# Attention stage of a hybrid layer: two output products of a tile to steps 59 and 61, and its second square, root, norm and row transposes later

## The chip, the cores and the metric

The kernel is one program on one core of a Trainium2 chip. The metric is the device time of one execution in microseconds. It computes a whole transformer layer: modulation, retention, attention, output projection and feed-forward. The engines are TensorE (PE in the profile, its weight loads PEld), VectorE (DVE), ScalarE (ACT), GpSimd (POOL) and SyncE (SP), which issues the transfers.

## The reference

The layer has 2048 rows of width 1024, 256 context rows, 4 retention heads and 8 attention heads in 2 groups of 4 (each group has one key and value head). What matters here is the line that joins the two halves, and the normalised row that the feed-forward reads:

```python
ret = _ret_out(ret, rg, ret_gn_g)                       # retention, normalised and gated, 512 wide
att = _latent_attention(q, k, v, kc, vc)                # softmax(q k^T / 8) v over 2304 keys, 512 wide
x = x + g1 * (jnp.concatenate([ret, att], axis=-1) @ w_out)
h2 = _modulate(_rmsnorm(x, norm2_g), sh2, sc2)          # x * rsqrt(mean(x^2) + eps) * g * (1 + sc2) + sh2
x = x + g2 * _sqrelu_mlp(h2, w_ff1, w_ff2)
return _rmsnorm(x, final_norm_g)
```

## The kernel before

The rows are 16 tiles of 128, worked from t = 15 down to t = 0. The attention stage is one long list of **steps**. A planner, `on(k, phase, fn, ...)`, files each piece of work under a step and a phase; the stage then runs through the steps, in each through the phases `begin, scores, piece, maximum, early, exp, cast, low, chain, pe, values, late, dma`, and each piece adds its instructions to its engines' queues. So the table of steps is the order on every engine, and every engine works strictly in that order. Engines wait for each other by semaphores alone.

A head group of a tile has 18 steps, a tile 36. In every step attention does the following, for keys in blocks of 128 or 512:

- **scores** (L210, L211): two matmuls, 128x512, into one of two PSUM buffers `st`
- **piece** (L177 or two L181): one matmul of the next group's plain scores into one of two buffers `mp`, whose row maximum VectorE takes one step later (L190)
- **exp** (L216): ScalarE, one step later, `st` to `p`; every second step **cast** (L220) makes the fp16 part `phi`
- **low** (L227 on GpSimd, whole, or L229 on VectorE, two halves): the rest `plo`
- **values** (L242 to L245): every second step, 16 small matmuls of `phi` and `plo` with the values into `o`; at a group's end ScalarE takes `o` to `so` (L249, L250) and GpSimd makes `ma` (L262, L263).

Around this stand the other jobs of a tile, each with steps of its own. Let k = 40 + 36 n for the n-th tile; "step 59" of a tile means k + 59. So step 59 of one tile is step 23 of the next.

- `retention`: score (bank 0) at 2 (38 of the tile before), heads at 6 to 9 (42 to 45), copy `oo` at 46, statistics at 48 and 49, a root on GpSimd (cv_gn, mr, cy_gn, mr), four norms on ScalarE (L1696) at 52 and 54, the gate (L1700); the decays oqf and oqb (L1652, GpSimd) at 68 and 69, and a weighing okw (L1628).
- `output_tile`: transposes of the retention half `oo` at 24 and of the attention half `ma` at 28 (L1816), each split into fp16 parts (`rh`, `rl`, `ah`, `al`); then 16 products (L1834 to L1836, three matmuls each), 8 for each half of the 1024 columns, at the steps of the table `PLACES`, accumulated in PSUM bank 0; per half an `add` to the row `xr` (L1841, VectorE) and a `square` with a row sum (L1848, ScalarE); then the row goes out (`store_x`), a `root` of the sums (a VectorE add L1855, then two small GpSimd operations cv_f and cy_f, which a list called `chain` hands out one after each of three phases), a `norm` of the row in place (L1861, GpSimd), eight transposes in two lots (L1866), `modulate` (L1871, VectorE), `shift_` (L1876, GpSimd) and two stores of the new row `h2`.
- `parts` and `turn` of attention: the row maxima of the next group go through three small GpSimd operations (mt, L198 to L200) at 50 and 68 into four VectorE transposes (L204) at 52 and 70.
- `h_pair`: from the eighth tile on, rows of finished tiles are read back and combined: GpSimd sums (L1933) and fp16 splits (ScalarE L72, GpSimd L73), more of them in every second tile, where a pair begins.

The last tile (t = 0) has a table of its own, `LAST`.

Of the kernel before, what the change touches and what calls it, by code (L numbers as in the profile page):

```python
# [56 lines left out]
def layer_kernel(ctx: ExitStack, tc: tile.TileContext, a: dict, out: bass.AP):  # L57
# [84 lines left out]
    early = kp.tile([P, NK * (VW + 1)], F32, name="early", tag="wv")  # L142
# [127 lines left out]
    with ExitStack() as st, tc.manual_schedule():  # L270
# [952 lines left out]
        for n, (col, s) in enumerate(((C_RK, 5), (C_AKV, 6), (C_AQ, 12), (C_RQ, 16), (C_RV, 18), (C_RG, 26))):  # L1223
            w = weights[0, col]
            for j in range(w.n):
                at = s + (j if col != C_RV else j > 0)
# [35 lines left out]
        at = [16, 17, 18, 19, 20, 20, 21, 21, 24, 25, 39, 40, 41, 42, 44, 46, 49, 50, 52, 54, 56, 58, 60, 62]  # L1262
# [3 lines left out]
        at = [39, 40, 41] + list(range(43, 64, 2)) + list(range(66, 84))  # L1266
        for i in range(32):
            greatest_of(i, at.pop(0))
        at = list(range(7, 18)) + list(range(36, 42)) + [43, 46, 50, 54, 57] + list(range(66, 84))
# [265 lines left out]
    def on(k, phase, fn, *args):  # L1535
        events.setdefault((k, phase), []).append((fn, args))
# [262 lines left out]
        on(k + 3, "pe", spread)  # L1799
        on(k + 3, "late", scales)  # L1800

    PLACES = (28, 29, 30, 31, 32, 33, 34, 35, 46, 48, 49, 50, 52, 54, 55, 57)
    LAST = (23, 24, 25, 26, 30, 31, 32, 33, 25, 26, 27, 28, 34, 34, 35, 35)

    def output_tile(t, k, last):
# [78 lines left out]
            on(k + at[1], "cast", part, w, 0)  # L1884
            on(k + at[2], "low" if last and w == "a" else "early", part, w, 1)
        on(k + 26, "dma", fetch_x)
        places = LAST if last else PLACES
        for j, at in enumerate(places):
            on(k + at, "pe", product, j // 8, j % 8)
        for n in range(2):  # L1890
            at = k + places[8 * n + 7] + 1
            on(at, "early", add, n)
            on(at if last else at + 1, "cast", square, n)
        made = at
        on(made + 1, "dma", store_x)
        on(made if last else made + 2, "late", root)
        on(k + 68 if t == 1 else made + 2 if last else made + 4, "late", norm)
        if last:
            for f in (transpose_x, modulate, shift_, store_h):
                rest.extend([(f, 0), (f, 1)])  # L1900
# [1 line left out]
        if t == 1:  # L1902
# [3 lines left out]
                on(k + 82 + q, "late", shift_, q)  # L1906
                on(k + 83 + q, "dma", store_h, q)
            return made
        on(k + 68, "pe", transpose_x, 0)
        on(k + 70, "early", modulate, 0)  # L1910
        on(k + 72, "pe", transpose_x, 1)
        on(k + 73, "early", modulate, 1)
        for q in range(2):
            on(k + 74 + q, "late", shift_, q)
            on(k + 76 + q, "dma", store_h, q)
        return made


# [40 lines left out]
    for n, t in enumerate(range(NT - 1, -1, -1)):  # L1959
        made_at = output_tile(t, R0 + RF * n, n == NT - 1)  # L1960
# [449 lines left out]
    with tc.manual_schedule():  # L2410
# [8 lines left out]
        k = min(events)[0]  # L2419
# [69 lines left out]
```

## Time and profile before

| | |
|---|---|
| median of 3 runs | 2636.21 us (2634.91 to 2636.67) |
| profiled execution, first to last instruction | 2633.9 us (its time is given as this span alone) |
| granted TensorE clock, mean | 0.999 |
| busy: TensorE / VectorE / ScalarE / GpSimd | 98% / 78% / 57% / 67% |
| matmuls | 16617 |
| attention stage, first to last L210 | 598.0 to 1443.8 us |

The profile is of one execution. Busy times are sums over the span. A timeline row has a start in us from the span's start, a duration in us, engine, line, operation, output<-input, shapes and a count of merged instructions, and in brackets the idle time before it with what ended it. A matmul row of 512 columns shows 0.38 us, but the next one starts 0.216 us later, since matmuls overlap; so distances are read from start to start.

### The profile page before, as it was taken

To read this page: it belongs to the slowest core of one execution; us is meant where nothing else is said; L and a number is where in the kernel's file an instruction comes from. 1 tells how busy PE (TensorE), PEld (TensorE's weight loads), DVE (VectorE), ACT (ScalarE), POOL (GpSimd) and SP (SyncE) were. 2 spreads that over 40 slices of the span, in tenths; PEclk is the share of its full clock that TensorE was granted. 3 is DMA by queue.
4 is the path that set the end of the run, shared out by engine and by line. 5 is a ranking of instruction groups with operands and counts; after the bars stand their busy time and mean duration, and the time that the engine had idled before them with its cause. 6 is when DMAs were issued, how large, how long until landed. Compare 5 with 4: busy or idle time off the path is not lost.

```text
span 2633.9 us, 45447 instructions
## 1 busy us (share of the span) xinstructions
PE 2594.3 (98%) x16617; PEld 1450.6 (55%) x16617; DVE 2043.7 (78%) x3080; ACT 1509.5 (57%) x2562; POOL 1762.5 (67%) x1451
## 2 busy tenths in 40 slices
PE   8999999998999999999999999999999999999998
PEld 5875555546666666666666444444444444444443
DVE  5688898668888888888887697889886666656686
ACT  3865453427777787888788476656665322222243
POOL 3644566536676678798887695777662566666686
PEclk9999999999999999999999999999999999999999
DMA  7776999736122132333322855777784748475453
GB/s 232 274 255 214 312 328 340 257 106 220 49 71 59 57 112 74 101 85 115 99 83 75 293 159 163 233 224 232 223 293 139 281 170 300 163 284 185 151 190 114
DMA packets 332903, 481.84 MB, mean 183 GB/s; under 512 B 90228, under 2 KB 200068, under 8 KB 328200
## 3 DMA queue, kind: packets, MB, share of 16 engines
q1 hardware_dynamic: 332664, 478.94, 55.2%
q8 instruction: 130, 2.13, 0.3%
q14 instruction: 93, 0.76, 0.1%
q10 hardware_dynamic: 16, 0.01, 0.0%
HBM read 321.89 MB, written 156.38 MB: 182 GB/s over the span
## 4 chain that ended last, share of the span: by engine, by line
PE 84%; DVE 5%; ACT 4%; DMA 3%; POOL 2%; issue 2%; SPq 0%; DVEq 0%; POOLq 0%; ACTq 0%
PE pd L2302 7%; PE pd L2300 7%; PE pd L2301 7%; PE pu L2073 7%; PE pu L2075 7%; PE pu L2074 7%; PE pso L1193 4%; PE pso L1195 4%; PE pso L1194 4%; PE st L210 4%; PE o L245 4%; PE st L211 4%; PE mp L177 3%; PE o L243 2%; PE bank L1836 2%; PE bank L1834 2%
## 5 line engine op out<-in xcount | busy, mean ns | idle before, releaser
L190 DVE TENSOR_REDUCE nm<-mp 128x1 f32<-128x512 f32 x558 | 377.7, 685 | 89.2 <-PE mp L177 83.7
L216 ACT ACTIVATE p<-st 128x512 f32<-128x512 f32 x576 | 341.1, 599 | 154.4 <-PE st L211 150.5
L227 POOL TENSOR_TENSOR plo<-p,phi 128x1024 f16<-128x1024 f32 x160 | 347.0, 2174 | 86.2 <-ACT phi L220 86.1
L2073 PE MATMUL pu<-hf,w1f 128*128 128x512 f16 x896 | 339.6, 379 | 1.5 <-ACT w1f L2049 0.9
L2075 PE MATMUL pu<-hf,w1f 128*128 128x512 f16 x896 | 339.6, 379 | 0.4 <-DVE w1f L2055 0.4
L2300 PE MATMUL pd<-w,uf 128*128 128x512 f16 x896 | 339.6, 379 | 0.0
L2302 PE MATMUL pd<-w,uf 128*128 128x512 f16 x896 | 339.6, 379 | 0.0
L2301 PE MATMUL pd<-w,uf 128*128 128x512 f16 x896 | 339.6, 379 | 0.0
L2074 PE MATMUL pu<-hf,w1f 128*128 128x512 f16 x896 | 339.6, 379 | 0.0
L2320 POOL TENSOR_TENSOR y<-y,d 128x512 f32<-128x512 f32 x128 | 210.5, 1647 | 146.6 <-ACT uf L2289 95.5
L220 ACT ACTIVATE phi<-p 128x1024 f16<-128x1024 f32 x288 | 305.1, 1059 | 0.0
L229 DVE TENSOR_TENSOR plo<-p,phi 128x512 f16<-128x512 f32 x256 | 236.3, 924 | 21.2 <-ACT phi L220 8.7
L243 PE MATMUL o<-wv,plo 128*128 128x65 f16 x2304 | 230.0, 193 | 0.0
L245 PE MATMUL o<-wv,phi 128*128 128x129 f16 x2176 | 228.3, 220 | 0.0
L210 PE MATMUL st<-qr,ks 128*128 128x512 f16 x576 | 218.0, 379 | 8.7 <-ACT p L216 6.2
L243 PEld LDWEIGHTS <-plo 128*128 128x128 f16 x2304 | 205.1, 98 | 28.5 <-issue 0.6
L2312 DVE SCALAR_TENSOR_TENSOR y<-pd,scy,y 128x512 f32<-128x512 f32 x160 | 116.9, 747 | 131.8 <-PE pd L2302 130.4
L211 PE MATMUL st<-qr,ks 128*128 128x512 f16 x576 | 218.2, 379 | 0.1
L2085 DVE TENSOR_TENSOR r<-pu,r 128x512 f32<-128x512 f32 x224 | 150.0, 684 | 82.7 <-PE pu L2075 56.8
L1193 PE MATMUL pso<-wf,h_l 128*128 128x512 f16 (+1 forms) x576 | 208.1, 361 | 0.0
L1195 PE MATMUL pso<-wf,h_l 128*128 128x512 f16 (+1 forms) x576 | 208.1, 361 | 0.0
L1194 PE MATMUL pso<-wf,h_l 128*128 128x512 f16 (+1 forms) x576 | 208.1, 361 | 0.0
(394 smaller groups left out, 6118.0 us busy)
## 6 DMA issues: line engine op xcount, KB each, us to landing
wm<-in_w_ff SPq DMA_DIRECT2D x64, 512.0 KB, 6.4
u<-r SPq DMA_DIRECT2D x128, 256.0 KB, 4.3
ur<-u SPq DMA_DIRECT2D x128, 256.0 KB, 5.8
y<-x SPq DMA_DIRECT2D x64, 512.0 KB, 6.2
wf<-w2f SPq DMA_DIRECT2D x112, 256.0 KB, 2.8
w<-wf SPq DMA_DIRECT2D x28, 1024.0 KB, 9.8
w1r<-in_w_ff SPq DMA_DIRECT2D x48, 512.0 KB, 5.3
x<-y SPq DMA_DIRECT2D x48, 512.0 KB, 2.6
```

Of the source, the lines that this page charges most:

```text
L190: nc.vector.tensor_reduce(dst, src, axis=AX.X, op=ALU.max, negate=True)
L211: mm(ps, ks2[:, self.g, k], q[:, 1], start=False, stop=True)
L216: nc.scalar.activation(self.p[kt // 2][:, kt % 2], self.s.pop(kt), AF.Exp, scale=HD**-0.5)
L227: nc.gpsimd.tensor_tensor(lo, p, hi, op=ALU.subtract)
L243: mm(o[:, : HD + 1], lo[:, i, c], v[:, : HD + 1], start=False, stop=False)
L245: mm(o, hi[:, i, c], v[:, :VW], start=False, stop=last)
L2073: mm(pu[hf, i], whi, hi, start=k == 0, stop=False)
L2074: mm(pu[hf, i], whi, lo, start=False, stop=False)
L2075: mm(pu[hf, i], wlo, hi, start=False, stop=k == 3)
L2300: mm(ps, u[:, 0, b], w[:, b, 0], start=b == 0, stop=False)
L2301: mm(ps, u[:, 0, b], w[:, b, 1], start=False, stop=False)
L2302: mm(ps, u[:, 1, b], w[:, b, 0], start=False, stop=b == 3)
```

## The change

`PLACES` loses the steps 49, 55 and 57 for the second half's products and gets 56, 59 and 61. What follows the last product is filed relative to it or set anew: the second half's add goes from 58 to 62, its square from 59 to 65, the row's store from 59 to 63, the root from 60 to 66, the norm from 62 to 68, the transposes from 68 and 72 to 70 and 74, modulate from 70 and 73 to 72 and 75, shift and stores by one step. The tile t = 1 keeps the old places (`LAST1`) with square and root two steps later; the last tile keeps its table.

```diff
-    PLACES = (28, 29, 30, 31, 32, 33, 34, 35, 46, 48, 49, 50, 52, 54, 55, 57)
+    PLACES = (28, 29, 30, 31, 32, 33, 34, 35, 46, 48, 50, 52, 54, 56, 59, 61)
+    LAST1 = PLACES[:8] + (46, 48, 49, 50, 52, 54, 55, 57)
...
-        places = LAST if last else PLACES
+        places = LAST if last else LAST1 if t == 1 else PLACES
...
-            on(at if last else at + 1, "cast", square, n)
+            on(at if last else at + 1 + 2 * n, "cast", square, n)
...
-        on(made if last else made + 2, "late", root)
-        on(k + 68 if t == 1 else made + 2 if last else made + 4, "late", norm)
+        on(made if last else made + 4, "late", root)
+        on(made + 2 if last else k + 68, "late", norm)
...
-        on(k + 68, "pe", transpose_x, 0)
-        on(k + 70, "early", modulate, 0)
-        on(k + 72, "pe", transpose_x, 1)
-        on(k + 73, "early", modulate, 1)
+        on(k + 70, "pe", transpose_x, 0)
+        on(k + 72, "early", modulate, 0)
+        on(k + 74, "pe", transpose_x, 1)
+        on(k + 75, "early", modulate, 1)
         for q in range(2):
-            on(k + 74 + q, "late", shift_, q)
-            on(k + 76 + q, "dma", store_h, q)
+            on(k + 75 + q, "late", shift_, q)
+            on(k + 77 + q, "dma", store_h, q)
```

Lines after the table are one number higher in the changed kernel (L1848 becomes L1849). On ScalarE, around steps 59 to 62 of the first tile, there stands before:

```order
L220 ACTIVATE phi<-p_8467 128x1024
L1848 ACTIVATE oat,ss<-xr 128x512
L216 ACTIVATE p_8508<-st 128x512
L249 ACTIVATE so<-o_8144 128x258
L250 ACTIVATE so<-o_8145 128x258
L216 ACTIVATE p_8558<-st 128x512
L220 ACTIVATE phi<-p_8508 128x1024
L216 ACTIVATE p_8558<-st 128x512
L1822 ACTIVATE rh<-bank_8543 128x512
```

and now, with the square (oat,ss) further down, between phi of step 65 and ah of step 66:

```order
L249 ACTIVATE so<-o_8144 128x258
L250 ACTIVATE so<-o_8145 128x258
L216 ACTIVATE p_8547<-st 128x512
L220 ACTIVATE phi<-p_8501 128x1024
L216 ACTIVATE p_8547<-st 128x512
L1823 ACTIVATE rh<-bank_8536 128x512
L216 ACTIVATE p_8603<-st 128x512
L220 ACTIVATE phi<-p_8547 128x1024
L216 ACTIVATE p_8603<-st 128x512
L216 ACTIVATE p_8654<-st 128x512
L220 ACTIVATE phi<-p_8603 128x1024
L1849 ACTIVATE oat,ss<-xr 128x512
```

The square has left the place between phi and the two so copies and stands six exponentials later. On GpSimd, steps 62 to 70 of the same tile, before (plo are the low parts, xr the norm):

```order
L227 TENSOR_TENSOR plo<-p_8508,phi 128x1024
L1861 TENSOR_SCALAR xr<-xr,cy_f 128x1024
L1628 TENSOR_TENSOR okw<-ork,kd 128x512
L227 TENSOR_TENSOR plo<-p_8612,phi 128x1024
L198 TENSOR_SCALAR mt_6726<-m_8742 128x4
L199 TENSOR_SCALAR m_8742<-m_8742 128x4
L200 TENSOR_TENSOR mt_6726<-m_8742,mt_6726 128x4
L1652 TENSOR_TENSOR oqf<-oqt,tf 128x512
L1652 TENSOR_TENSOR oqb<-oqt,tb 128x512
```

and now:

```order
L227 TENSOR_TENSOR plo<-p_8501,phi 128x1024
L1628 TENSOR_TENSOR okw<-ork,kd 128x512
L227 TENSOR_TENSOR plo<-p_8603,phi 128x1024
L1556 TENSOR_SCALAR cv_f<-ss 128x1
L1557 TENSOR_TENSOR cy_f<-cv_f,half 128x1
L198 TENSOR_SCALAR mt_6726<-m_8741 128x4
L199 TENSOR_SCALAR m_8741<-m_8741 128x4
L200 TENSOR_TENSOR mt_6726<-m_8741,mt_6726 128x4
L1652 TENSOR_TENSOR oqf<-oqt,tf 128x512
L1862 TENSOR_SCALAR xr<-xr,cy_f 128x1024
L1652 TENSOR_TENSOR oqb<-oqt,tb 128x512
```

The norm has gone from behind plo of step 62 to between oqf and oqb, and the two root operations stand right ahead of mt. On TensorE, step 61 (scores, piece, then the values of the next group) has now, with the last product of the tile (ah, al) between piece and values:

```order
L210 MATMUL st<-qr,ks 128x512
L211 LDWEIGHTS ks_6720
L211 MATMUL st<-qr,ks_6720 128x512
L177 LDWEIGHTS qr
L177 MATMUL mp<-ks,qr 128x512
L1835 LDWEIGHTS ah
L1835 MATMUL bank_8220<-wo,ah 128x512
L1836 LDWEIGHTS ah
L1836 MATMUL bank_8220<-wo,ah 128x512
L1837 LDWEIGHTS al
L1837 MATMUL bank_8220<-wo,al 128x512
L242 LDWEIGHTS phi
```

Before, the rows from L177 go straight to L242, and this product stands in step 57.

## The prediction

> **What bounds the kernel now.** I read the page's busy shares first, then the waits of TensorE, then the timeline of one tile's period in the attention stage, engine by engine. All times are of the profiled execution, whose span is 2633.9 us; the median of the runs is 2636.21 us, 2.3 us (0.09%) above it. A difference below 0.2% (5.3 us) cannot be told from no change with this kernel.
>
> ```profile
> PE 2594.3 (98%) x16617; PEld 1450.6 (55%) x16617; DVE 2043.7 (78%) x3080; ACT 1509.5 (57%) x2562; POOL 1762.5 (67%) x1451
> ...
> PE st L210 <- ACT p L216: 4.6, 15, 0.3
> ...
> 660.00:1445.00 785.00, 777.79 (x7442) 515.89 (x7442) 674.60 (x1215) 628.24 (x1048) 609.05 (x528) 1.00 0.28 82
> ```
>
> The first row is the page's. The second is the waits of TensorE from 665 to 1445 us, the stage with the change (us in total, times, longest): scores waiting for an exponential, 15 times 0.3 us. The third is that stage by engine: busy us of PE, weight loads, DVE, ACT, POOL, then a granted clock of 1.00. TensorE is close to full, so nothing here can win more than its few waits, and moved matmuls win nothing by themselves. What a wait costs is read from the starts of L210, one per step. Rows without a wait give the measure:
>
> ```profile
> 1001.43 0.38 PE L210 MATMUL st<-qr,ks 128*128 128x512 f16 x1
> 1002.08 0.38 PE L210 MATMUL st<-qr,ks 128*128 128x512 f16 x1
> ...
> 982.74 0.60 PE L1816 MATMUL bank<-ident,ma 128*128 128x128 f32 x4
> 983.17 0.38 PE L1834 MATMUL bank<-wo,rh 128*128 128x512 f16 x1
> 983.82 0.38 PE L210 MATMUL st<-qr,ks 128*128 128x512 f16 x1
> ```
>
> A step with scores and piece alone lasts 1002.08 - 1001.43 = 0.65 us; four transposes add 983.17 - 982.74 = 0.43, one output product (L1834 to L1836) adds 0.65, and an odd step's value matmuls bring it to about 1.35. Now steps 60 to 63 of one tile (TensorE and ScalarE, one timeline):
>
> ```profile
> 976.08 1.05 ACT L220 ACTIVATE phi<-p 128x1024 f16<-128x1024 f32 x1
> 976.89 0.38 PE L210 MATMUL st<-qr,ks 128*128 128x512 f16 x1
> 977.03 0.62 ACT L1848 ACTIVATE oat<-xr 128x512 f32<-128x512 f32 x1
> 977.64 0.58 ACT L216 ACTIVATE p<-st 128x512 f32<-128x512 f32 x1
> 978.12 0.38 ACT L249 ACTIVATE so<-o 128x258 f32<-128x258 f32 x1
> 978.28 0.38 PE L210 MATMUL st<-qr,ks 128*128 128x512 f16 x1
> 978.65 0.61 ACT L216 ACTIVATE p<-st 128x512 f32<-128x512 f32 x1
> 979.13 1.08 ACT L220 ACTIVATE phi<-p 128x1024 f16<-128x1024 f32 x1
> 979.62 0.38 PE L210 MATMUL st<-qr,ks 128*128 128x512 f16 x1
> 980.08 0.62 ACT L216 ACTIVATE p<-st 128x512 f32<-128x512 f32 x1
> 980.55 0.63 ACT L1822 ACTIVATE rh<-bank 128x512 f16<-128x512 f32 x1
> 980.75 0.38 PE L210 MATMUL st<-qr,ks 128*128 128x512 f16 x1 [0.32 <-ACT p L216]
> ```
>
> There are two score buffers, so the L210 of a step starts when the exponential of two steps earlier is done: 977.64 + 0.58 = 978.22 lets 978.28 go, 980.08 + 0.62 = 980.70 lets 980.75 go. Step 60 lasts 978.28 - 976.89 = 1.39 us where scores, piece and transposes take 0.65 + 0.43 = 1.08; step 62 lasts 980.75 - 979.62 = 1.13 where 0.65 would do. The loss is 0.31 + 0.48 = 0.79 us per tile. The first part is no idle row, because the transposes' modelled ends cover it.
>
> ScalarE is the cause. Start to start, an exponential p takes 0.48, phi 0.95, the square L1848 0.61, the two so copies 0.53, rh 0.48. From step 58 to 62 it has five p, two phi, so and rh, 5.3 us, and the square makes it 5.9, while TensorE without waits passes these steps in 0.65 + 1.35 + 1.08 + 1.35 + 0.65 = 5.1. The difference of 0.8 is the stall.
>
> **The change part by part.** *Second square to step 65, two products to 59 and 61.* ScalarE's 5.3 us now meet TensorE steps of 0.65 + 2.0 + 1.08 + 2.0 + 0.65 = 6.4 us. Both waits go: 0.79 us in each of 14 tiles (the tile t = 1 keeps its places and the last has its own table), 14 x 0.79 = 11.0 us. At its new place the square meets steps 64 to 67, which last 0.65 + 0.43 + 0.65, 2.0, 1.3 and 2.0, together 7.0 us, and ScalarE has four p, two phi, ah and the square there, 4.9 us; no score should wait. The products themselves are the same 48 matmuls per tile in a different order: nothing.
>
> *Products taken away from 49, 55 and 57.* They were cover. In ordinary tiles no wait stands there. In each second tile from the eighth on, where h_pair begins a pair (four tiles), one does:
>
> ```profile
> L1696 ACT ACTIVATE oo<-oo,mr,cy_gn 128x128 f32<-128x128 f32 x64 | 28.0, 488 | 7.8 <-POOL mr L1690 7.8
> ...
> 1118.53:1127.86 9.33, 9.33 (x84) 5.47 (x83) 8.56 (x22) 6.54 (x10) 9.08 (x12) 1.00 0.15 31
> ...
> 1127.66 0.20 POOL L1690 TENSOR_TENSOR mr<-mr,cy_gn 128x4 f32<-128x4 f32 x1
> 1127.70 0.38 PE L210 MATMUL st<-qr,ks 128*128 128x512 f16 x1
> 1127.89 0.88 ACT L1696 ACTIVATE oo<-oo,mr,cy_gn 128x128 f32<-128x128 f32 x2 [1.47 <-POOL mr L1690]
> 1128.68 0.57 ACT L216 ACTIVATE p<-st 128x512 f32<-128x512 f32 x1
> 1129.30 0.38 PE L210 MATMUL st<-qr,ks 128*128 128x512 f16 x1
> ```
>
> GpSimd works without a gap from 1118.53, the beginning of step 46, to mr (the second row: 9.08 of 9.33 us busy). ScalarE waits 1.47 us for mr before the retention's norm L1696; the p behind it ends at 1129.25 and the L210 of step 54 at 1129.30 has waited 1129.30 - 1127.70 - 1.35 = 0.25 us. GpSimd's queue there is unchanged, so this p ends as late after step 46 as now, but TensorE arrives 0.65 us sooner, since the product at 49 is gone. The wait grows by 0.65: 4 x 0.65 = 2.6 us lost. In the tiles between, ScalarE waits for mr too (7.8 us in all, less 4 x 1.47, leaves 0.47 each); the scores there have some slack left and I put nothing; the bounds are 0 and another 0.65 in four tiles.
>
> *Norm (L1861) from 62 to 68, first transposes from 68 to 70.* This is the only place where the change shortens a distance: 6 steps become 2. The norm leaves GpSimd's queue after low of step 62 and stands between oqf and oqb of step 68:
>
> ```profile
> L1861 POOL TENSOR_SCALAR xr<-xr,cy_f x16: 1116/1124/1558, 716.4 to 1478.3; 128x1024 f32<-128x1024 f32 x16
> ...
> 1202.83 0.38 PE L210 MATMUL st<-qr,ks 128*128 128x512 f16 x1
> 1203.14 0.24 POOL L198 TENSOR_SCALAR mt<-m 128x4 f16<-128x4 f32 x1 [1.86 <-DVE m L194]
> 1203.92 1.27 POOL L1652 TENSOR_TENSOR oqf<-oqt,tf 128x512 f32<-128x512 f32 x1
> 1204.28 1.47 DVE L229 TENSOR_TENSOR plo<-p,phi 128x512 f16<-128x512 f32 x1
> 1205.16 1.72 POOL L1652 TENSOR_TENSOR oqb<-oqt,tb 128x512 f32<-128x512 f32 x1
> 1206.55 0.38 PE L210 MATMUL st<-qr,ks 128*128 128x512 f16 x1
> ...
> 658.04 1.72 POOL L1700 TENSOR_TENSOR oo<-oo,ogate 128x512 f32<-128x512 f32 x1
> ...
> 659.81 0.44 PE L1816 MATMUL bank<-ident,oo 128*128 128x128 f32 x2 [1.24 <-POOL oo L1700]
> ```
>
> Step 68 begins at 1202.83. The 1.86 us idle before mt take in the two small root operations. The norm starts where oqb starts, 1205.16. oqb took 1.72 there against 1.27 for the like oqf, because the L229 that began under oqf was still running: 0.45 us longer. The norm's 1.12 becomes 1.56 (its own maximum, 1558 ns) and ends at 1206.72. TensorE wants it in step 70, which begins 0.43 sooner than in the row, at 1206.12, since its transposes have left step 68; after scores and piece it is 1206.77. The last two rows show how fast TensorE follows GpSimd: oo ends at 659.76, the transposes start at 659.81. So the first transpose starts on time, but its weight load is not hidden under the matmul ahead of it, and I put 0.06 us per tile: 14 x 0.06 = 0.8 us. The bounds are 0 (the norm at 1.12, ending at 1206.28) and 0.5 (half a microsecond late, one more short operation ahead of it on GpSimd); the value is near the lower one, because it rests on rows of the same slot. In the four tiles where h_pair adds a form and a sum to GpSimd ahead of this, its slack before mt is a few tenths only; I put another 0.2 each, 0.8 us (0 to 0.5 each).
>
> The Trainium skill, SBUF — State Buffer, section "SBUF: two separate sides", says that VectorE and GpSimd have one pair of SBUF ports in common, an exclusive lock: a VectorE operation with two SBUF inputs and a GpSimd operation that reads SBUF never run together, and the later one waits for the whole of the other. The trace agrees (1.72 against 1.27 us, and 1.47 for an L229). It speaks against the new slot; with it the sum below is 6.8 us, without it 7.6.
>
> *What is moved besides.* oqb follows the norm and low of steps 70 and 72 come about 1.1 us later; oqb has until step 78, low three steps (over 4 us). store_x goes to 63, behind three loads of the next tile on SP, and SP then waits for the add of step 62 before it issues the query loads of step 64; oqf reads them late in step 68, some 8 us on, and twice their size lands in 6.2 (median, the page's DMA part): nothing.
>
> ```profile
> y<-x SPq DMA_DIRECT2D x64, 512.0 KB, 6.2
> ```
>
> The shift and its stores are one step later, with no reader in the stage nearby. The add of step 62 frees the bank two steps before its next product at 64: nothing. For t = 1 the root comes two steps later, its norm stays: nothing.
>
> Sum: 11.0 - 2.6 - 0.8 - 0.8 = 6.8 us less. The span goes to 2627.1, the median to 2636.2 - 6.8 = **2629.4 us**, 0.26% faster.
>
> **Rivals.** *Slower: the norm becomes the wait.* If mt or the root chain comes late at step 68 (m on VectorE behind the root's add, which waits for the square on ScalarE), the norm, and with it TensorE, is late by as much in all 14 tiles. For it: 2 steps' distance and an order that VectorE must keep. Against: the square ends near step 66's start, and GpSimd has 1.86 us idle ahead of mt. From 0.55 us per tile (0.06 and 6.8 / 14) it eats the gain; one L229 length, 1.47 us, would make 14 x 1.41 - 6.8 = 13 us more, 2649; about 0.9 us, 2641. *No change: less than the stall goes, or more cover is lost.* If only the wait of step 62 went, and so and rh kept the other alive, the gain would be 14 x 0.48 = 6.7 less 4.2, 2.5 us: 2633.7. The same comes out if the tiles between lose 0.65 too and the norm is 0.2 late. For it: both waits stand around so and rh, too. Against: 5.3 us of work in 6.4. *All of it:* the retention's wait is repaid by GpSimd running ahead, the norm is never late: 11.0 us, 2625.2. Against: mr is bound by GpSimd's queue alone.
>
> **How the numbers follow.** My forecast, with 5.3 to 9 us gained, has 0.46; nearly all of the stall gained 0.11; a gain below 5.3 us or a loss of as much 0.35; slower 0.08. That gives faster 0.57, same 0.35, slower 0.08. The range that leaves out 2 in 10 is 2625.2 (all of the 11.0) to 2635.5 (0.7 us gained, half of the no-change cases beyond the 2.5).
>
> **What would show it.** L210 waits for p hardly at all in ordinary tiles, and their period falls by 0.7 us; ScalarE's idle time before L1696 grows from 7.8 us towards 10.4 and the L210 behind it waits 0.9 us in four tiles; the norm starts behind oqf and ends 3.9 us after the L210 of step 68, oqb is back at 1.27. I am wrong if TensorE waits for xr by more than a tenth in ordinary tiles, or if L210 waits for p at a new place.

## The result, and the profile after

The changed kernel takes 2669.53 us (median of 4 runs, 2666.91 to 2673.04) against 2636.44 us of the kernel before on the same chip (4 runs, 2634.91 to 2640.06). The ratio is 1.0124, with a 95% interval of 1.0112 to 1.0136: 33 us slower, where 7 us less were forecast. The profiled execution has a span of 2669.1 us; its first L210 starts 1.6 us later than before.

The rows that answer to the first ones shown of before: the page's busy times, the waits of TensorE in the attention stage (us in total, times, longest), and the stage by engine. The stage now ends later, so the windows reach to 1480 us.

```profile
PE 2602.4 (98%) x16617; PEld 1449.9 (54%) x16617; DVE 2071.7 (78%) x3080; ACT 1511.6 (57%) x2562; POOL 1763.0 (66%) x1451
```

```profile
PE mp L177 <- DVE nm L190: 20.6, 16, 1.6
PE bank L1867 <- POOL xr L1862: 4.0, 5, 1.2
PE bank L1634 <- PE mp L177: 3.5, 13, 0.3
PE st L210 <- ACT p L216: 2.0, 5, 0.5
```

```profile
660.00:1480.00 820.00, 788.20 (x7466) 517.20 (x7465) 704.86 (x1220) 635.42 (x1055) 612.54 (x530) 1.00 0.27 79
```

The wait that the change was about has gone from the ordinary tiles: nearly all that is left in the last row stands at step 54 of four h_pair tiles. In its place stands a wait that the kernel before did not have: the piece matmul L177 waits for VectorE's row maximum L190, 20.6 us in all, and in 13 tiles the matmul behind it, L1634, another 0.27 us. VectorE is 28 us busier (2071.7 against 2043.7) with the same 3080 instructions, so some of them have become longer.

**Where the time went.** I subtracted the distances between consecutive L210 of before from those of after, for each step and tile, and added them over the tiles. Steps into or out of which matmuls move are taken together.

| place | us in all | per tile |
|---|---|---|
| steps 60 and 62 (exponential) | -10.9 | -0.30 and -0.48 in 14 |
| step 77, with 78 | +32.1 | +2.22 in 11 of 13, 3.8 in two |
| step 70 (norm) | +6.3 | +0.15 in nine, 1.0 to 1.4 in the four where h_pair begins a pair, 0.7 in the last |
| steps 53 to 56 (mr) | +1.6 | 0.35 in four |
| step 59 | +2.0 | 0.31 and 0.20 in h_pair tiles |
| before the first tile, step 67 | +1.9 | |
| sum | +33.0 | |

**Step 77.** One tile's steps 74 to 77, first before, then after, TensorE, VectorE and GpSimd in one timeline. Two low parts stand here: one on VectorE in two halves (L229, steps 74 and 75) and one whole on GpSimd (L227, step 76); u<-u,s is the shift, u<-bank,a is modulate.

```profile
1104.15 2.08 POOL L1876 TENSOR_TENSOR u<-u,s 128x512 f32<-128x512 f32 x2
1105.63 1.15 DVE L229 TENSOR_TENSOR plo<-p,phi 128x512 f16<-128x512 f32 x1
...
1107.30 0.68 DVE L229 TENSOR_TENSOR plo<-p,phi 128x512 f16<-128x512 f32 x1
...
1107.75 2.22 POOL L227 TENSOR_TENSOR plo<-p,phi 128x1024 f16<-128x1024 f32 x1 [1.52 <-ACT phi L220]
...
1108.94 0.38 PE L210 MATMUL st<-qr,ks 128*128 128x512 f16 x1
...
1111.18 0.38 PE L210 MATMUL st<-qr,ks 128*128 128x512 f16 x1
```

```profile
1123.00 1.04 POOL L1877 TENSOR_TENSOR u<-u,s 128x512 f32<-128x512 f32 x1
1123.01 1.57 DVE L229 TENSOR_TENSOR plo<-p,phi 128x512 f16<-128x512 f32 x1
...
1125.11 0.68 DVE L1872 TENSOR_TENSOR u<-bank,a 128x512 f32<-128x512 f32 x1
...
1125.59 2.12 POOL L227 TENSOR_TENSOR plo<-p,phi 128x1024 f16<-128x1024 f32 x1 [1.55 <-ACT phi L220]
1125.71 2.55 DVE L229 TENSOR_TENSOR plo<-p,phi 128x512 f16<-128x512 f32 x1
...
1126.77 0.38 PE L210 MATMUL st<-qr,ks 128*128 128x512 f16 x1
...
1128.18 0.68 DVE L190 TENSOR_REDUCE nm<-mp 128x1 f32<-128x512 f32 x1
...
1128.92 0.38 PE L177 MATMUL mp<-ks,qr 128*128 128x512 f16 x1 [1.55 <-DVE nm L190]
...
1131.23 0.38 PE L210 MATMUL st<-qr,ks 128*128 128x512 f16 x1
```

Before, the second L229 starts 0.45 us ahead of GpSimd's L227 and takes 0.68; L227 takes 0.1 more than its usual 2.12. After, modulate (L1872) stands ahead of it, it comes 0.12 us behind L227, and takes 2.55 us: 2.00 until L227 has ended at 1127.71, and then some 0.55 of its own. The row maximum behind it starts at 1128.18, TensorE, with both buffers mp taken, waits 1.55 us, and step 77 lasts 1131.23 - 1126.77 = 4.46 instead of 2.24 us. The Trainium skill, SBUF — State Buffer, section "SBUF: two separate sides", says that of such a pair whichever starts first keeps the port for its whole instruction. The trace agrees here: being 0.12 us late costs VectorE 1.9 us.

**Step 70 in an h_pair tile**, GpSimd, one row of VectorE (m, the row maxima that mt reads) and TensorE after the change. The L210 of step 70 is at 1172.83.

```profile
1169.56 0.52 POOL L1556 TENSOR_SCALAR cv_f<-ss 128x1 f32<-128x1 f32 x1
...
1169.95 0.16 DVE L194 TENSOR_REDUCE m<-nm 128x4 f32<-128x20 f32 x1
...
1170.17 0.58 POOL L1557 TENSOR_TENSOR cy_f<-cv_f,half 128x1 f32<-128x1 f32 x1
...
1170.83 0.24 POOL L198 TENSOR_SCALAR mt<-m 128x4 f16<-128x4 f32 x1
...
1173.25 1.12 POOL L1862 TENSOR_SCALAR xr<-xr,cy_f 128x1024 f32<-128x1024 f32 x1
...
1174.42 0.44 PE L1867 MATMUL bank<-ident,xr 128*128 128x128 f32 x2 [0.79 <-POOL xr L1862]
```

GpSimd has no gap over 0.1 us here, and the two small root operations take 1170.83 - 1169.56 = 1.27 us of its queue, while m is ready at 1169.95 + 0.16 = 1170.11. So they hold mt, and with it the norm, 0.72 us back in this trace. That they are the cause is not shown, though: in e5 below the root stands at step 60 as before, and in the same tile TensorE waits 0.83 us for the norm. There mt waits 0.72 us for m, which is ready 1.27 us after the L210 of step 68 instead of 0.58. In both kernels the norm starts 3.7 us after that L210, against 2.4 in an ordinary tile.

### The profile page after: what moved, and what is told of

Read it like the earlier page. It is cut to its first block, busy times and chain, and to the rows that moved or that the text cites. A ratio compares the mean times of both kernels' runs of the same rounds, so it can differ in the third digit from the quotient of the medians.

```text
span 2669.1 us, 45441 instructions
## 1 busy us (share of the span) xinstructions
PE 2602.4 (98%) x16617; PEld 1449.9 (54%) x16617; DVE 2071.7 (78%) x3080; ACT 1511.6 (57%) x2562; POOL 1763.0 (66%) x1451
## 4 chain that ended last, share of the span: by engine, by line
PE 79%; DVE 9%; POOL 4%; DMA 4%; ACT 2%; issue 2%; SPq 0%; DVEq 0%; POOLq 0%; ACTq 0%
PE pd L2301 7%; PE pd L2303 7%; PE pd L2302 7%; PE pu L2074 7%; PE pu L2076 7%; PE pu L2075 7%; PE pso L1193 4%; PE pso L1194 4%; PE pso L1195 4%; PE o L245 3%; PE st L210 3%; PE st L211 3%; PE mp L177 3%; DVE plo L229 3%; PE o L243 2%
## 5 line engine op out<-in xcount | busy, mean ns | idle before, releaser
L190 DVE TENSOR_REDUCE nm<-mp 128x1 f32<-128x512 f32 x558 | 377.1, 684 | 93.4 <-PE mp L177 85.0
L227 POOL TENSOR_TENSOR plo<-p,phi 128x1024 f16<-128x1024 f32 x160 | 345.3, 2163 | 93.4 <-ACT phi L220 93.3
L229 DVE TENSOR_TENSOR plo<-p,phi 128x512 f16<-128x512 f32 x256 | 252.4, 987 | 21.3 <-ACT phi L220 13.0
L210 PE MATMUL st<-qr,ks 128*128 128x512 f16 x576 | 218.8, 380 | 3.7 <-ACT p L216 3.6
L177 PE MATMUL mp<-ks,qr 128*128 128x512 f16 x512 | 194.4, 380 | 24.9 <-DVE nm L190 23.1
L1193 PE MATMUL pso<-wf,h_l 128*128 128x512 f16 (+1 forms) x576 | 208.4, 362 | 0.0
L1194 PE MATMUL pso<-wf,h_l 128*128 128x512 f16 (+1 forms) x576 | 208.3, 362 | 0.0
```

Of the source, the lines that this page charges most:

```text
L190: nc.vector.tensor_reduce(dst, src, axis=AX.X, op=ALU.max, negate=True)
L227: nc.gpsimd.tensor_tensor(lo, p, hi, op=ALU.subtract)
L229: nc.vector.tensor_tensor(lo[:, i], p[:, i], hi[:, i], op=ALU.subtract)
L1193: mm(ps[:, :width], hi[:, k], wh, start=k == 0, stop=False)
```

## Experiments

Step figures below are again differences of the distances between L210 against before. The kernel before was run beside each kernel, and its median lay between 2636.66 and 2637.79 us.

**e1, the second modulate behind VectorE's low.**

```diff
-        on(k + 75, "early", modulate, 1)
+        on(k + 76, "early", modulate, 1)
```

> The changed kernel with the second modulate filed one step later (76 instead of 75), so that VectorE runs the second half of the pair's low part (L229) ahead of it; nothing else. Theory A (lock): the 2.2 us that each tile loses in step 77 come from this modulate, which pushes L229 0.6 us back, behind the start of GpSimd's low part (L227) of step 76; L229 then waits for the whole of it (2.55 us against 0.68), the next row maximum comes late and TensorE's piece waits. Expected 2637 us (2634 to 2640), L229 there back at about 0.7 us. Rival B (TensorE's order): the second transposes in step 74, beside the retention's scores, make the mask and the product of step 77 late. Expected unchanged, 2669. Rival C (norm): the norm in GpSimd's queue at step 68 makes its later low parts late. Expected unchanged, 2669.

Measured: 2639.22 us, ratio 1.0013 (1.0004 to 1.0023). Step 77 loses 0.34 us per tile instead of 2.22. The pair of rows shows why:

```profile
1109.26 0.68 DVE L229 TENSOR_TENSOR plo<-p,phi 128x512 f16<-128x512 f32 x1
1109.74 2.19 POOL L227 TENSOR_TENSOR plo<-p,phi 128x1024 f16<-128x1024 f32 x1 [1.55 <-ACT phi L220]
```

L229 is 0.48 us ahead again. One instruction of 0.6 us, moved behind another, gives back 30 us.

**e3, GpSimd's low one step later** (the first pair of the second head group), with modulate left where the change puts it.

```diff
-                    on(k + 2 * j + 4, "low", g.low, j)
+                    on(k + 2 * j + (5 if n % 2 and j == 0 else 4), "low", g.low, j)
```

> The changed kernel with GpSimd's low part of the first pair of each odd group one step later (77 instead of 76), behind both shifts; modulate, transposes and norm stay as changed. Theory A: L229 finds the ports free or waits for a shift alone (1.0 us instead of 2.1), so most of the 32 us goes: 2638 us (2634 to 2645). Rival B: unchanged, 2669. Rival C: GpSimd has as much to do ahead of it: unchanged, 2669, or worse, as the low part is a step nearer to its values.

Measured: 2640.79 us, ratio 1.0015 (1.0006 to 1.0024), step 77 again +0.34. VectorE does here all that it does in the changed kernel, in the same order; only GpSimd comes later. So it is not modulate's own 0.6 us on VectorE that costs 2.2 us, but who is first.

**e2, the transposes' part alone:** the kernel before with transposes at 70 and 74, modulate at 72 and 75, shift and stores one step later. Products, square, root and norm stay.

> The kernel before with one part of the change alone: row transposes at 70 and 74, modulate at 72 and 75, shift at 75 and 76, stores at 77 and 78; products, second square, root and norm as before. Theory A: the collision is there without the rest, 2.2 us in 14 tiles: 2667 us (2660 to 2670), with the waits of the scores for the exponential still there. Rival B: the same, about 2667. Rival C: unchanged from before, 2636.

Measured: 2640.11 us, ratio 1.0017 (1.0008 to 1.0027). Theory A failed here, and B with it: modulate stands ahead of the second L229, and yet step 77 loses only 0.22 us. The timeline of the same steps:

```profile
1107.34 1.04 POOL L1876 TENSOR_TENSOR u<-u,s 128x512 f32<-128x512 f32 x1
1108.36 0.69 DVE L229 TENSOR_TENSOR plo<-p,phi 128x512 f16<-128x512 f32 x1
...
1110.32 0.69 DVE L1871 TENSOR_TENSOR u<-bank,a 128x512 f32<-128x512 f32 x1 [0.64 <-PE bank L1866]
1110.93 2.67 POOL L227 TENSOR_TENSOR plo<-p,phi 128x1024 f16<-128x1024 f32 x1 [2.55 <-ACT phi L220]
1110.93 0.68 DVE L229 TENSOR_TENSOR plo<-p,phi 128x512 f16<-128x512 f32 x1
```

Here GpSimd's shift ends (1108.38) as the first L229 starts, which takes 0.69 us; in the changed kernel the shift starts 0.01 us ahead of it and it takes 1.57. So VectorE is 0.88 us earlier, even waits 0.64 us for the transposes, and the second L229 starts level with L227 and wins. A second ingredient was missing: what makes the shift late? The norm, now 1.1 us of GpSimd's queue ahead of it (theory A2), or the moved products with their add and square (D).

**e5, e2 with the norm at 68 as well**, and nothing else.

```diff
-        on(k + 68 if t == 1 else made + 2 if last else made + 4, "late", norm)
+        on(made + 2 if last else k + 68, "late", norm)
```

> The kernel before with the transposes' part and the norm at step 68 (root, square and products stay at their old steps). Theory A2: the collision at step 77 needs two things, modulate ahead of VectorE's low and the norm's 1.1 us on GpSimd, which pushes the shift of half 0 onto VectorE's earlier low. Then step 77 loses some 2.2 us per tile again (32), step 70 some 6, and the stalls at 60 and 62 stay: 2675 us (2665 to 2682). Rival D: the second thing is the moved products with their add and square on VectorE and ScalarE. Then this stays near the run with the transposes alone: 2640 to 2646 us.

Measured: 2676.59 us (2675.72 to 2686.56), ratio 1.0159 (1.0139 to 1.0180). The loss is back, without a product, a square or a root moved: step 77 and 78 cost 32.1 us, step 70 5.8, and the stalls at 60 and 62 remain. The rows are those of the changed kernel again:

```profile
1128.55 1.05 POOL L1876 TENSOR_TENSOR u<-u,s 128x512 f32<-128x512 f32 x1
1128.57 1.57 DVE L229 TENSOR_TENSOR plo<-p,phi 128x512 f16<-128x512 f32 x1
...
1131.14 2.13 POOL L227 TENSOR_TENSOR plo<-p,phi 128x1024 f16<-128x1024 f32 x1 [1.54 <-ACT phi L220]
1131.27 2.55 DVE L229 TENSOR_TENSOR plo<-p,phi 128x512 f16<-128x512 f32 x1
```

**e6, the changed kernel with the shifts behind GpSimd's low.**

```diff
-            on(k + 75 + q, "late", shift_, q)
-            on(k + 77 + q, "dma", store_h, q)
+            on(k + 76 + q, "late", shift_, q)
+            on(k + 78 + q, "dma", store_h, q)
```

> The changed kernel with GpSimd's two shifts one step later still (76 and 77), so that the first falls behind GpSimd's low of step 76. A2: the earlier low on VectorE is no longer held up by the shift, modulate and the later low come 0.9 us sooner, the later low starts ahead of GpSimd's, and step 77 loses 0.2 to 0.3 us per tile instead of 2.2: 2641 us (2637 to 2646). D: VectorE is late for another reason, the lock is lost as before: 2664 to 2670 us.

Measured: 2640.11 us, ratio 1.0006 (0.9997 to 1.0015), step 77 +0.22 per tile as in e2. Its first L229 takes 0.69 us:

```profile
1107.02 0.69 DVE L229 TENSOR_TENSOR plo<-p,phi 128x512 f16<-128x512 f32 x1
...
1109.59 0.68 DVE L229 TENSOR_TENSOR plo<-p,phi 128x512 f16<-128x512 f32 x1
1109.59 2.68 POOL L227 TENSOR_TENSOR plo<-p,phi 128x1024 f16<-128x1024 f32 x1 [2.54 <-ACT phi L220]
```

With e5 and e6, A2 is shown from both sides, and D falls: two locks in a chain, the first (shift against L229) making VectorE late enough to lose the second (L227 against L229). Each link alone costs little: with the first lock lost and the second won (e1 and e3, first L229 about 1.57 us, second 0.68) 0.34 us per tile, with modulate ahead and the first lock avoided (e2 and e6) 0.22.

**e4, the norm at 67 as well** (on e1), to price the other losses.

```diff
-        on(made + 2 if last else k + 68, "late", norm)
+        on(made + 2 if last else k + 68 if t == 1 else k + 67, "late", norm)
```

> The second modulate at 76 as in the first of these runs, and the norm at 67 instead of 68, ahead of the parts (mt) and the decay oqf in GpSimd's queue. If the 6.3 us that the changed kernel loses in step 70 are TensorE's wait for the norm (0.15 us in ten tiles, 1.0 to 1.4 in the four where a pair of h_pair begins), they go as well: 2631 us (2628 to 2634). If in those four tiles the norm then delays mt, and with it VectorE's transposes for the next group, they stay as another wait: 2635 to 2638.

Measured: 2635.19 us, ratio 0.9996 (0.9987 to 1.0005), 1.2 us above the range expected; the span is 2630.9. The loss of step 70 is gone to the last hundredth. The gain of 10.9 us is intact, but 5.0 at step 77 (0.27 in ordinary, 0.65 in four tiles), 2.0 at 59 and 1.5 at 53 to 56 eat most of it.

**e7, product 49 kept and 56 given up**, on e4 with the shifts of e6.

```diff
-    PLACES = (28, 29, 30, 31, 32, 33, 34, 35, 46, 48, 50, 52, 54, 56, 59, 61)
+    PLACES = (28, 29, 30, 31, 32, 33, 34, 35, 46, 48, 49, 50, 52, 54, 59, 61)
```

> Norm at 67, second modulate at 76, shifts at 76 and 77, and products 48, 49, 50, 52, 54, 59, 61 (49 kept, 56 given up): the waits behind the retention's norm no longer grow (1.7 us back) and step 77 loses at most 0.2 per tile (up to 3 us back); from 2635.2 us with norm and modulate alone to 2631 (2629 to 2635). If GpSimd's shift does not matter where modulate is already at 76, and the wait for mr is repaid elsewhere: 2635 us.

Measured: 2635.20 us, ratio 0.9993 (0.9984 to 1.0001): no gain over e4. Step 53 loses nothing now, but 56 loses 0.65 us in four tiles and 0.10 in four (3.0 in all). TensorE comes to mr's wait one product sooner in either case, though that step 56 still pays for mr is argued from the queues and not shown by a run of its own. With the cover at 49 instead of 56 the loss only moved, and grew from 1.5 to 3.0 us.

**e8, the last products at 57 and 60**, else as e7 (`..., 54, 57, 60`).

> As the run with 49 kept, but the last two products at 57 and 60. If the square was what made the stall, one product between the two value steps and one step of cover more ahead of step 59 are enough: the stall at 60 and 62 stays away and the 0.2 to 0.3 us at step 59 in the h_pair tiles go too: 2629 us (2627 to 2634). If the two products at 59 and 61 are needed as well, 0.3 to 0.5 us per tile come back at step 62: 2635 us (2633 to 2639).

Measured: 2646.46 us, ratio 1.0034 (1.0021 to 1.0047), far above both expectations. The stalls of 60 and 62 are gone and step 59 loses nothing, as expected. But add, square and root come one step sooner, and in the four h_pair tiles, where GpSimd has no gap, L227 of step 72 now holds up the first L229 and L227 of step 76 the second (step 73 +1.05, step 77 with 78 +2.3 to 4.0). What on GpSimd moved them together was not separated.

```profile
1161.90 2.15 POOL L227 TENSOR_TENSOR plo<-p,phi 128x1024 f16<-128x1024 f32 x1
1162.52 2.07 DVE L229 TENSOR_TENSOR plo<-p,phi 128x512 f16<-128x512 f32 x1
...
1165.02 2.13 POOL L227 TENSOR_TENSOR plo<-p,phi 128x1024 f16<-128x1024 f32 x1 [0.98 <-ACT phi L220]
1165.12 2.58 DVE L229 TENSOR_TENSOR plo<-p,phi 128x512 f16<-128x512 f32 x1
```

**e9 and e10, one product moved.** Norm at 67, transposes at 70 and 72, modulate at 72 and 73, shifts and stores as before; the second half's products at 46, 48, 49, 50, 52, 54 and then 55, 61 (e9) or 57, 61 (e10).

> Only one product moves (57 to 61), square 65, root 66, norm 67; transposes 70 and 72, modulate 72 and 73, shifts and stores at their places of before. Theory: the square is the stall, the four other losses are cover (49, 55) and the late second modulate. All of 11 us are gained, step 77 and the wait for mr cost nothing, step 59 up to 1 us: 2627 us (2625 to 2631). If the order of VectorE after the norm's slot flips a lock again, 2632 or more, with the loss at one of the steps 72 to 77.

> As the run with 57 to 61 alone, but 55 given up and 57 kept. The wait for mr shows at step 56 in the h_pair tiles as in the run with 49 kept, 3.0 us, step 59 loses nothing: 2629 us (2627 to 2633). If cover at 55 does not matter: 2626 us.

Measured: e9 2632.70 us, ratio 0.9983 (0.9974 to 0.9992); e10 2632.23 us, 0.9983 (0.9974 to 0.9992). Both keep the whole 10.9 us and lose only 1.7 at step 77. e10 pays 3.0 for mr at step 56, as expected, and 1.2 at 67; e9 pays some 5 in crumbs of 0.1 to 0.4 at 58, 59, 64 and 67. So the medians gain 4.4 and 4.9 us, some half of what was expected. The 0.13 us at step 67 in nine tiles stand behind a lost lock: there the L229 of step 65 takes 2.24 to 2.57 us, as long as the one that costs the changed kernel 2.2 us a tile.

**e11, the square alone:** the kernel before with the second square at 63, root at 64, norm at 66, no product moved.

```diff
-            on(at if last else at + 1, "cast", square, n)
+            on(at if last else at + 1 + 4 * n, "cast", square, n)
...
-        on(made if last else made + 2, "late", root)
-        on(k + 68 if t == 1 else made + 2 if last else made + 4, "late", norm)
+        on(made if last else made + 6, "late", root)
+        on(k + 68 if t == 1 else made + 2 if last else made + 8, "late", norm)
```

> The kernel before with the second square at 63, the root at 64 and the norm at 66, no product moved. If the square alone makes the stall, ScalarE's 5.3 us against TensorE's 5.1 leave 0.2 of 0.79 us per tile, nothing else is touched: 14 x 0.55 = 8 us less, 2629 us (2626 to 2633). If the two products between the value steps are needed as well, the waits of 60 or 62 stay at 0.3 or more per tile: 2632 to 2637 us. A norm late for step 68 in the h_pair tiles would add up to 1 us in each of four.

Measured: 2641.43 us, ratio 1.0020 (1.0011 to 1.0029), slower where a gain was expected. The stalls shrink by 0.30 and 0.30 us in all 14 tiles, 8.5 us: the square alone made most of the stall, and a product moved to 59 to 61 adds only the remaining 0.18 at step 62. Yet in the four h_pair tiles the norm comes behind GpSimd's low and ends at 1151.65, 3 us after step 68 began, and steps 68 and 69 lose 14.9 us together, more than the waits of TensorE (8.9); the last section has the rest:

```profile
1147.99 2.12 POOL L227 TENSOR_TENSOR plo<-p,phi 128x1024 f16<-128x1024 f32 x1
1148.67 0.38 PE L210 MATMUL st<-qr,ks 128*128 128x512 f16 x1
...
1150.10 1.55 POOL L1861 TENSOR_SCALAR xr<-xr,cy_f 128x1024 f32<-128x1024 f32 x1
1151.71 1.10 PE L1866 MATMUL bank<-ident,xr 128*128 128x128 f32 x4 [2.23 <-POOL xr L1861]
```

**e12, e11 with the norm at 65** (`made + 7`), ahead of that low.

> As the run with the square at 63 and no product moved, but the norm at 65, ahead of GpSimd's sum and low of step 66. There the norm came late for step 68 in the four h_pair tiles and cost 14.9 us. If GpSimd's queue was all, that loss goes, low of 66 comes as late as in the kernel before, and the 8.5 us of the stall remain as a gain: 2628 us (2625 to 2631). If low of 66 or another lock on VectorE takes up the norm's 1.1 us, it costs 0.2 to 2 us a tile at steps 68 to 71: 2632 to 2650 us.

Measured: 2631.44 us (2629.15 to 2635.43), ratio 0.9982 (0.9972 to 0.9991). The norm is done 1.3 us before the transposes of step 68, which follow the piece matmul without a wait:

```profile
1145.42 1.13 POOL L1861 TENSOR_SCALAR xr<-xr,cy_f 128x1024 f32<-128x1024 f32 x1
...
1147.61 0.38 PE L177 MATMUL mp<-ks,qr 128*128 128x512 f16 x1
1147.83 0.60 PE L1866 MATMUL bank<-ident,xr 128*128 128x128 f32 x4
```

It keeps the 8.5 us and loses 3.4, all in the h_pair tiles (0.5 at step 77, 0.2 to 0.45 at 69, 0.1 at 63). With e9 and e10 it is one of three versions whose interval lies below 1; 0.17 to 0.18% is about the least that can be told from no change with this kernel.

## Why the prediction was wrong, point by point

- **The step that failed is "What is moved besides ... nothing".** It followed the shift to its readers and asked whether it would be late, and it did not mention the second modulate, which moves from 73 to 75, at all; it did not ask what the two would stand against on the other engine's side of the lock. The lock was weighed for the norm's slot alone (0.45 us). That "low of steps 70 and 72 come about 1.1 us later" was right, but the shift behind them in the same queue comes later too. In its place the runs showed +32.1 us at step 77: the norm pushes the shift onto VectorE's first low, modulate and that delay push the second low behind GpSimd's (e5 and e6). The rows for it were there before: the second L229 led L227 by 0.45 us, modulate is 0.6 us long, and the first L229 already showed 1.15 instead of 0.68 us under the shift.
- **The stall, -11.0 us: right.** Measured -10.9: 0.30 us per tile at step 60 and 0.48 at step 62. Steps 60 and 62 of the tile shown in the prediction now last 990.78 - 989.70 = 1.08 and 993.42 - 992.77 = 0.65 us, without a wait:

```profile
989.70 0.38 PE L210 MATMUL st<-qr,ks 128*128 128x512 f16 x1
990.78 0.38 PE L210 MATMUL st<-qr,ks 128*128 128x512 f16 x1
992.77 0.38 PE L210 MATMUL st<-qr,ks 128*128 128x512 f16 x1
993.42 0.38 PE L210 MATMUL st<-qr,ks 128*128 128x512 f16 x1
```

  The cause given, ScalarE's square, holds: moving it alone gives 8.5 of it and leaves 0.18 us per tile (e11), as 5.3 us of ScalarE's work against TensorE's 5.1 would have it.
- **Products taken away, +2.6 us: place right, size a little high.** Steps 53 to 56 lost 1.6; 0.35 per tile, not 0.65. "GpSimd's queue there is unchanged" did not hold: mr ends 9.73 us after the L210 of step 46 instead of 10.03, because mt (L198), ahead of it in the queue, takes 0.24 instead of 0.55 us. Why mt is shorter was not tried. (The 1118.53 of the prediction is 0.70 us behind that L210; nothing hangs on it.) ScalarE's idle time before L1696 went from 7.8 to 11.7 us, where 10.4 was foreseen:

```profile
  POOL mr L1690: 11.7, 8
```

  The 2.0 us at step 59, where a row maximum comes late once the products of 55 and 57 no longer stand ahead, were not foreseen; with 57 kept they are gone (e8 and e10).
- **The norm, +0.8 and +0.8 us: the second term was mis-sized.** In ordinary tiles it was 0.15 (0.06 forecast, bounds 0 and 0.5). In the four h_pair tiles it was 1.0 to 1.4 (0.2 forecast, bound 0.5): the prediction read that GpSimd's "slack before mt is a few tenths only" and put no more than that against it, where the norm starts 1.3 us later after the L210 of step 68 than in ordinary tiles. The root operations in the queue are not needed for that: without them, in e5, the row maxima m come late by as much. The last tile lost 0.7. Together 6.3 us; one step earlier it costs nothing (e4).
- **The rivals.** The kernel came out slower, but not by "the norm becomes the wait": that wait is real, 4.0 us on TensorE, but step 70 took only 6.3 of the 10.9 us gained. As written, the rival looked for a late reader of the norm; the loss began at the shift, four operations behind the norm in the same queue. The prediction's signs of being wrong, TensorE waiting for xr in ordinary tiles or L210 for p at a new place, did not cover it either: the new wait is L177's for the row maximum.

## What to carry to other kernels

When an instruction is moved on VectorE or GpSimd, list what runs on the other of the two engines in the new slot and behind it, and note by how many tenths each pair of low, shift and norm leads: a lead smaller than the operation put ahead of it can turn into a wait for one whole operation of the other engine. What it costs the kernel depends on who waits behind it (2.2 us a tile at step 77, 0.13 at step 67 in e9), so try each part alone and in pairs: the transposes' part cost 3 us at step 77, with the norm's new slot 32. And before moving covered work, ask which single instruction makes the wait: moving the square with root and norm and no product (e12) gave as much as the best versions that move a product too (e9 and e10).

## What the runs showed of the hardware

**A lost lock costs the rest of the other engine's operation, and less than a tenth of a microsecond decides it.** L229 took 0.68 us when it started level with L227 (13 tiles each of e2 and e6), and 2.55 to 2.59 when it started 0.09 to 0.13 us behind it (after, e5, e8). Who starts first cannot be read to the hundredth: against the norm, L229 started 0.05 us later in four tiles of e8 and still took 0.68 us, with the norm at 1.65; against the shift it started 0.01 us later in the changed kernel and took 1.57.

**A wait of TensorE can halve the clock of the matmuls behind it, and where the wait falls decides it.** In two of the thirteen tiles of the changed kernel step 77 with 78 lost 3.8 us instead of 2.2. TensorE waited there as in the others, but then ran at half its clock for 3.41 us, from 742.88 and from 1186.61 on. Three windows of 3.41 us (busy us of PE, weight loads, DVE, ACT, POOL, then the granted clock):

```profile
739.46:742.87 3.41, 1.59 (x10) 0.96 (x9) 3.41 (x5) 1.85 (x3) 2.17 (x2) 1.00 0.12 42
742.88:746.29 3.41, 3.41 (x25) 2.71 (x24) 1.20 (x3) 1.49 (x4) 0.64 (x1) 0.50 0.61 176
...
1408.48:1411.89 3.41, 1.76 (x14) 0.72 (x11) 3.41 (x4) 2.05 (x4) 3.17 (x2) 1.00 0.00 0
```

The first holds the 1.55 us and the 0.27 us behind them whole, 3.41 - 1.59 = 1.82 us idle, and half clock follows. In the third, of another tile, the same two waits leave 1.65 us in the window and the rest in the next, and full clock follows. The spells of half clock start whole multiples of 3.413 us apart (742.88 and 1186.61 are 130 of them apart), so each trace has a fixed grid of such windows. From 660 us on, up to the last 15 us of each of the 14 traces, half clock followed each of the eight windows with 1.82 us of idle TensorE or more (after and e5 two each, e8 one, e11 three) and none of those with 1.77 or less. In e11, where TensorE waited 2.23 us, this took three of four tiles from 2.5 to 4.1 us, which is why steps 68 and 69 lost 14.9 us with 8.9 us of waiting. The Trainium skill, TensorE: Matmul & The Clock Gate, section "Part 1: The HAM clock gate", has the clock halved after an idle window of about 3.4 us that runs freely. The free-running window is seen here; but it need not be idle throughout, since 1.82 of 3.41 us were enough.
